# Projection stores on ScalarE's own queue, more buffers, another order of projection rows, and layer 2's S5 tables built inside the first MLP

## The chip, the cores and the metric

The kernel runs on one core of one Trainium2 chip. The metric is the device time of one execution in microseconds (us), lower is better; the time of a kernel is the median of its runs. PE is TensorE, PEld its weight loads, DVE is VectorE, ACT ScalarE, POOL GpSimd, SP SyncE, the engine that in the kernel before issues every DMA.

## What is computed

Two layers of a hybrid backbone block on 256 context and 1024 latent tokens of width 1024, all in float32. Each layer normalises and modulates its input, projects it once to four groups of heads, runs the four mixers in both directions, concatenates, projects back, adds, and then does the same with an MLP:

```python
pc, pl = split_cols(hc @ w_in), split_cols(hl @ w_in)
a = hgrn2_mixer(...)                       # gated linear attention, chunks of 16
r = retention_mixer(...)                   # rope, fixed decays, chunks of 64
g = gdn_mixer(...)                         # conv, then a triangular solve per chunk of 64
s = s5_mixer(...)                          # complex diagonal scan, 16 groups of 64 states
y = concatenate([a, r, g, s]) @ w_out
x = x + gate * y
x = x + gate2 * (square(relu(h2 @ w1)) @ w2)
```

The S5 scan of the reference is `h_t = a h_(t-1) + B u_t`, `y_t = Re(C h_t) + d u_t` for every group. It depends on the tokens only through u; B scaled by the step, the powers of a and the phasors depend on parameters alone.

## The kernel before, in words

Every dense product is made float32-exact by splitting each operand into a high and a low part and adding three matmuls (hi*hi, lo*hi, hi*lo). ACT makes the high parts, DVE or POOL the low parts (`w_lo`, `hlo`). A scheduler places the instructions: the program is written as generators with priorities, the scheduler estimates times and fixes an order for each engine, and every engine then runs its queue in that order. Work with priority (the mixers, inside `hi()`) comes as early as its inputs allow, and the "filler" of projections takes what is left of PE.

A layer has these stages. **Front**: `proj_steps` (L1642) computes rows of the input projection, each product being 24 matmuls into a PSUM tile `pj_ps` (L1661), copied to an SBUF tile `pj_z` by `evict` (L1634; every fourth copy on DVE, L1637, the others on ACT, L1639), and stored to memory from there by SP (L1666). `k.nz` = 3 buffers of pj_z, and the PSUM bank class 'mm' with 2 banks, bound how many copies are under way. The first rows are `k.rowsA`: 16, 14, 17, 15, 18, 19 are keys, queries and values of the gated DeltaNet, and row 'h' holds its decays and betas; the rest, `k.rowsB`, is filler. Beside it run `gdn_conv` (L596: convolution on DVE, L635, silu on ACT, L641, transposes to `gd_pt` on PE, L656, key products, stores of `gd_x` and `gd_tk` by SP), `gdn_stats` (L705, needs row 'h') and `s5_tables` (L1202). **GDN core**: `gdn_main` (L780) loads decays (`gd_E`, `gd_ge`, L804), forms the matrices `gd_M` and `gd_A`, solves the triangular systems on DVE (L864, L865) through the memory tile `lanes`, builds inverses (`gd_py`, L897) and steps along the chunks. **Mixers**: outputs of the DeltaNet, retention, HGRN2 and S5, woven with the next modulation. **S5**: `s5` (L1310) takes the tables `s5t` in four quarters: a product `s_px` (PE), a rotation by phasors, scans on DVE (L1380), a rotation back to `s_h`, products `s_py`; then a gelu and a gate (`s_pg`). **w_out**: `wo_ps` (L1521), first the six k-tiles of the other mixers, added on DVE (L1780), then the two S5 tiles. **MLP**: `mlp` (L1801) with `up_ps` and `dn_ps` back to back on PE; after each output tile it asks the filler for a step, and the filler is empty here.

`s5_tables(l)` (L1202) makes, in four iterations of four groups, the five tables of a quarter: EIN (DVE L1244 and L1246, POOL L1245, four transposes `s_pe` on PE, L1249), CA (L1254 to L1256), products `s_pm` (PE, L1260) that become a Toeplitz table by way of memory, and the phasors PC and PS by doubling (L1301 to L1303): each step computes the next m entries from those that are there, with the cosines on DVE and the sines on POOL, each needing the other's previous step. It is run in the front of its own layer, layer 0's as well as layer 1's.

Of the kernel before, what the change touches and what calls it, by code (L numbers as in the profile page):

```python
# [1201 lines left out]
def s5_tables(k, l):  # L1202
# [5 lines left out]
    for qi in range(4):  # L1208
        q4 = slice(4 * qi, 4 * qi + 4)
        fr, fi = (s[n].rearrange('p (l d g) -> p l d g', l=2, d=2)[:, l, :, q4] for n in ('fr', 'fi'))  # L1210
        uc, us = (s[n].rearrange('p (l d g) -> p l d g', l=2, d=2)[:, l, :, 2 * qi:2 * qi + 2] for n in ('uc', 'us'))
        own = [tile_('s5_tb', [128, b - a], f's5_tb{i}') for i, (a, b) in enumerate(zip(TBO, TBO[1:]))]
        EIN, PC, PS, CA, TP = s5_views(own)
        store = lambda i: nc.sync.dma_start(k.s5t[l][qi, :, TBO[i]:TBO[i + 1]], own[i])
        XP = tile_('s5_xp', [128, 2, 2, 4, 9], bufs=2)
# [6 lines left out]
        BR = tile_('s5_BR', [128, 2, 4, 16])
        BI = tile_('s5_BI', [128, 2, 4, 16])
        B2 = tile_('s5_B2', [128, 2, 4, 16])
        tq = tile_('s5_tq', [128, 4, 16])
        sh = [128, 4, 16]
        for d in range(2):
            f_r, f_i = bc(fr[:, d, :, None], sh), bc(fi[:, d, :, None], sh)
            V.tensor_tensor(BR[:, d], br, f_r, op=MULT)
            V.tensor_tensor(tq, bi, f_i, op=MULT)  # L1230
            V.tensor_tensor(BR[:, d], BR[:, d], tq, op=SUB)
            V.tensor_tensor(BI[:, d], bi, f_r, op=MULT)
            V.tensor_tensor(tq, br, f_i, op=MULT)
            V.tensor_tensor(BI[:, d], BI[:, d], tq, op=ADD)
# [3 lines left out]
        pts = []  # L1238
        for d in range(2):
            ee = tile_('s5_ee', [128, 4, 8, 16])  # L1240
            et = tile_('s5_et', [128, 4, 8, 16], 's5_et', 2)
            pw = lambda a: (rev(a[:, d, :, 0:8], 2) if d == 0 else a[:, d, :, 0:8])[:, :, :, None]
            sh = [128, 4, 8, 16]
# [13 lines left out]
            ps = mx(k, 's5_pm')  # L1257
            for g in range(2):
                for y in range(2):
                    nc.tensor.matmul(ps[64 * y:64 * y + 16, g * 128:g * 128 + 128], B2[:, d, 2 * g + y],  # L1260
                                     CA[:, d, 2 * g + y, 1 - d:9 - d].rearrange('p t c -> p (t c)'), start=True, stop=True)
            pts.append(ps)
            yield
        store(0)
        store(3)
        MB = tile_('s5_mb', [128, 2, 240])
        for r in Y2:
            q = slice(r.start, r.start + 16)
            f_ = pts[0][q, 0:256].rearrange('p (g c) -> p g c', g=2)
            b_ = pts[1][q, 0:256].rearrange('p (g c) -> p g c', g=2)  # L1270
            nc.scalar.activation(MB[q, :, 0:128], f_, AF.Copy)
            nc.scalar.activation(MB[q, :, 128:240], b_[:, :, 16:128], AF.Copy)
            V.tensor_tensor(MB[q, :, 112:128], MB[q, :, 112:128], b_[:, :, 0:16], op=ADD)
            for g in range(2):
                V.scalar_tensor_tensor(MB[q, g, 112:128], k.c['dmask'][q, 0:16], s['d'][q, l, 2 * qi + g:2 * qi + g + 1],
                                       MB[q, g, 112:128], op0=MULT, op1=ADD)
# [4 lines left out]
        for y in range(2):
            for g in range(2):
                t = toep[y, :, g]
                nc.sync.dma_start(TP[:, g, y], bass.AP(tensor=t.tensor, offset=t.offset,
                                                       ap=[[16, 8], list(t.ap[0]), [1, 128]]))
        G.memset(PC[:, :, :, 0], 1.0)
        G.memset(PS[:, :, :, 0], 0.0)
        G.tensor_copy(PC[:, :, :, 1], uc)
        G.tensor_copy(PS[:, :, :, 1], us)
        store(4)  # L1290
        f8 = lambda a: a.rearrange('p d g n -> p (d g) n')
        n = 1
        while n < NB - 1:
            m = min(n, NB - 1 - n)
            sh = [128, 4, m]
# [2 lines left out]
            for e, t, x, a, y, b, op in ((V, PC, xr, ar, xi, ai, SUB), (G, PS, xr, ai, xi, ar, ADD)):
                w = tile_('s5_pq', [128, 4, 64], 's5_pv' if e is V else 's5_pg')[:, :, :m]
                o = f8(t)[:, :, n + 1:n + m + 1]  # L1300
                e.tensor_tensor(o, x, a, op=MULT)  # L1301
                e.tensor_tensor(w, y, b, op=MULT)
                e.tensor_tensor(o, o, w, op=op)  # L1303
# [338 lines left out]
def proj_steps(k, l, H, rows, need_ctx):  # L1642
# [9 lines left out]
    def product(row, W, b0, bn, n, dst):  # L1652
# [214 lines left out]
def program(k):  # L1867
    from contextlib import ExitStack
    nc, tc = k.nc, k.tc
    with ExitStack() as es:  # L1870
# [62 lines left out]
        for l in range(2):  # L1933
# [104 lines left out]
def tune(k):  # L2038
# [63 lines left out]
```

## Time and profile before

| | us |
|---|---|
| median of 3 runs | 3759.85 (3757.71 to 3773.92) |
| profiled execution | 3765.0, span 3763.2, mean granted clock 0.935 |
| setup | 0 to 80 |
| layer 0: front and GDN core, mixers, S5 with w_out, MLP | 80, 717, 953, 1143 to 2030 |
| layer 1: front and GDN core, mixers, S5 with w_out, MLP | 2040, 2603, 2858, 3034 to 3763 |
| PE, DVE, ACT, POOL busy | 3337.9, 2072.9, 1110.0, 1143.3 |

The second row is one execution with the profiler on; all rows of the trace belong to it. Busy shares are means over stages, so each stage has to be read by itself. The granted clock is the share of full speed that PE was given.

### The profile page before, as it was taken

What the parts mean: (1) busy time and instruction counts of PE and PEld (TensorE: products, weight loads), DVE (VectorE), ACT (ScalarE), POOL (GpSimd) and SP (SyncE); (2) the same over time, 40 slices, a digit from 0 to 9 for tenths busy, and PEclk for the clock granted to TensorE, in tenths of its full rate; (3) what the DMA queues carried; (4) which work ended last, traced back from release to release, by engine and by line L of the source; (5) the groups of instructions that cost most, each with busy time, mean ns of one, the idle gap of its engine ahead of it and who ended that gap; (6) DMA issues with size and microseconds to landing.
All of it is one profiled execution on the core that took longest, in us unless ns stands there. A gap on an engine that the chain in (4) does not pass through costs nothing.

```text
span 3763.2 us, 60098 instructions
## 1 busy us (share of the span) xinstructions
PE 3337.9 (89%) x23367; PEld 2711.3 (72%) x23367; DVE 2072.9 (55%) x3927; ACT 1110.0 (29%) x1988; POOL 1143.3 (30%) x1198
## 2 busy tenths in 40 slices
PE   5884999897889999999997884999688799999997
PEld 3674788655767888888886784778456578888886
DVE  8958441587765334334436978421876654344445
ACT  5333212365243121121123333122462232222222
POOL 3724222364213111111112744222552231111111
PEclk8987899999999999999998997999798899999998
DMA  6547444775531111111112566534946311111111
GB/s 211 185 137 184 144 126 131 228 251 184 172 134 37 37 37 40 40 40 36 38 40 86 165 179 168 148 115 136 290 134 207 113 43 48 48 48 45 51 45 65
DMA packets 423949, 429.45 MB, mean 114 GB/s; under 512 B 185968, under 2 KB 299504, under 8 KB 422640
## 3 DMA queue, kind: packets, MB, share of 16 engines
q1 hardware_dynamic: 423664, 425.61, 36.3%
q8 instruction: 184, 3.01, 0.3%
q14 instruction: 101, 0.83, 0.1%
HBM read 313.26 MB, written 112.22 MB: 113 GB/s over the span
## 4 chain that ended last, share of the span: by engine, by line
PE 58%; DVE 11%; DMA 5%; issue 2%; ACT 2%; SPq 1%; POOL 1%; DVEq 0%; POOLq 0%; ACTq 0%
PE dn_ps L1521 21%; PE up_ps L1521 21%; PE pj_ps L1661 6%; PE wo_ps L1521 4%; DMA w_mo<-in_mod_w 1%; PE hg_pa L171 1%; DVE nm_u L1624 1%; DVE gd_y L635 1%; DVE hlo L1631 1%; PE mod_ps L1545 0%; DVE gd_tmp L864 0%; DVE s_x L1380 0%; DMA at<-a 0%; DVE hg_t L221 0%; DVE nr_acc L1593 0%
## 5 line engine op out<-in xcount | busy, mean ns | idle before, releaser
L1521 PE MATMUL dn_ps<-hid,w_hi 128*128 128x512 f32 (+1 forms) x2560 | 726.9, 373 | 9.0 <-DVE x L1833 7.7
L1833 DVE SCALAR_TENSOR_TENSOR x<-dn_ps,mod,x 128x512 f32<-128x512 f32 (+1 forms) x640 | 433.1, 695 | 323.2 <-PE dn_ps L1521 322.7
L1506 POOL TENSOR_TENSOR w_lo<-w_st,w_hi 128x512 fp32r<-128x512 f32 (+1 forms) x212 | 283.9, 1341 | 1044.1 <-ACT w_hi L1503 1016.2
L1521 PEld LDWEIGHTS dn_ps<-hid,w_hi 128*128 128x128 f32 x2560 | 462.8, 189 | 98.8 <-DVE x L1833 9.1
L1503 ACT ACTIVATE w_hi<-w_st 128x512 fp32r<-128x512 f32 (+2 forms) x408 | 249.8, 621 | 804.7 <-PE dn_ps L1521 275.7
L1521 PE MATMUL up_ps<-hlo,w_hi 128*128 128x512 f32 (+1 forms) x1280 | 475.6, 372 | 3.4 <-DVE hlo L1631 1.9
L1521 PE MATMUL up_ps<-hhi,w_hi 128*128 128x512 f32 (+1 forms) x1280 | 476.3, 373 | 2.0 <-ACT hhi L1630 2.0
L1521 PE MATMUL up_ps<-hhi,w_lo 128*128 128x512 f32 (+1 forms) x1280 | 475.8, 372 | 0.0
L1521 PE MATMUL dn_ps<-hid,w_lo 128*128 128x512 f32 (+1 forms) x1280 | 468.5, 373 | 0.0
L1661 PE MATMUL pj_ps<-hhi,w_hi 128*128 128x512 f32 (+1 forms) x960 | 366.5, 383 | 37.8 <-ACT pj_z L1639 28.0
L1661 PE MATMUL pj_ps<-hhi,w_lo 128*128 128x512 f32 (+1 forms) x960 | 365.3, 381 | 0.6 <-POOL w_lo L1506 0.6
L1661 PE MATMUL pj_ps<-hlo,w_hi 128*128 128x512 f32 (+1 forms) x960 | 363.8, 379 | 1.8 <-DVE hlo L1631 1.8
L1818 POOL TENSOR_TENSOR up_q<-up_r 128x256 f32<-128x256 f32 (+1 forms) x160 | 156.0, 976 | 565.5 <-ACT up_r L1817 476.9
L1506 DVE TENSOR_TENSOR w_lo<-w_st,w_hi 128x512 fp32r<-128x512 f32 (+1 forms) x196 | 148.6, 763 | 306.8 <-ACT w_hi L1503 298.3
L1521 PEld LDWEIGHTS up_ps<-hlo,w_hi 128*128 128x128 f32 x1280 | 242.3, 189 | 49.0 <-DVE hlo L1631 3.5
L1521 PEld LDWEIGHTS up_ps<-hhi,w_hi 128*128 128x128 f32 x1280 | 242.2, 189 | 46.2 <-ACT hhi L1630 2.8
L1521 PEld LDWEIGHTS up_ps<-hhi,w_lo 128*128 128x128 f32 x1280 | 242.0, 189 | 44.0
L1521 PEld LDWEIGHTS dn_ps<-hid,w_lo 128*128 128x128 f32 x1280 | 240.3, 189 | 45.6
L1820 DVE TENSOR_TENSOR hid<-up_q,hid 128x256 fp32r<-128x256 f32 (+1 forms) x160 | 114.3, 723 | 278.4 <-ACT hid L1819 276.0
L1661 PEld LDWEIGHTS pj_ps<-hhi,w_hi 128*128 128x128 f32 x960 | 189.7, 198 | 73.3 <-ACT pj_z L1639 29.6
L1819 ACT ACTIVATE hid<-up_q 128x256 fp32r<-128x256 f32 (+1 forms) x160 | 89.2, 584 | 423.2 <-PE dn_ps L1521 337.4
L1661 PEld LDWEIGHTS pj_ps<-hlo,w_hi 128*128 128x128 f32 x960 | 189.9, 198 | 33.1 <-DVE hlo L1631 2.4
(401 smaller groups left out, 5871.9 us busy)
## 6 DMA issues: line engine op xcount, KB each, us to landing
w_st<-in_w SPq DMA_DIRECT2D x256, 256.0 KB
w_mo<-in_mod_w SPq DMA_DIRECT2D x160, 256.0 KB
w_st<-in_w_ch SPq DMA_DIRECT2D x88, 256.0 KB
z<-pj_z SPq DMA_DIRECT2D x88, 256.0 KB
gd_KV<-kv SPq DMA_DIRECT2D x80, 192.0 KB
s_ta<-s5t SPq DMA_DIRECT2D x8, 1152.0 KB
w_mo<-in_mod_w SPq DMA_DIRECT2D x16, 512.0 KB
at<-a SPq DMA_DIRECT2D x32, 256.0 KB
```

Source lines behind the costliest of these rows:

```text
L171: m = nc.tensor.matmul(ps[Y2[c % 2], o:o + 128], key[:, a:a + 64], z[:, :, q:q + 64], start=True, stop=True)
L635: nc.vector.scalar_tensor_tensor(o, xl[:, r0 + a - 1:r1 + a - 1, w0 + b - 1:w1 + b - 1], w(a, b), o, op0=MULT, op1=ADD)
L1503: nc.scalar.activation(fl(hi), fl(st), AF.Copy)
L1506: eng.tensor_tensor(fl(lo), fl(st), fl(hi).bitcast(F32), op=SUB)
L1521: k.nc.tensor.matmul(out, w, x, start=(i + j == 0), stop=(i == n - 1 and j == 2))
L1624: nc.vector.scalar_tensor_tensor(u, X(kt)[:, sl], a, rb[:, :bn], op0=MULT, op1=MULT)
L1631: nc.vector.scalar_tensor_tensor(lo[:, sl], u, b, hi[:, sl].bitcast(F32), op0=ADD, op1=SUB)
L1661: nc.tensor.matmul(ps[:, :n], x, y, start=(kt == 0 and i == 0), stop=(kt == 7 and i == 2))
L1818: nc.gpsimd.tensor_tensor(q[:, :bn], r[:, :bn], r[:, :bn], op=MULT)
L1819: nc.scalar.activation(hi[:, sl], q[:, :bn], AF.Copy)
L1820: nc.vector.tensor_tensor(lo[:, sl], q[:, :bn], hi[:, sl].bitcast(F32), op=SUB)
L1833: nc.vector.scalar_tensor_tensor(X(m)[:, sl], ps[:, :bn], g, X(m)[:, sl], op0=MULT, op1=ADD)
```

## The change

1. `evict` gets the destination and issues the store itself: ACT's copies are stored from ACT's queue, DVE's from SP's as before.
2. `k.nz` 3 to 6, the projection's PSUM classes ('mm',) to ('mm', 'mm', 'mo') (three banks rather than two), `gd_E` 2 to 4 buffers, `gd_tk` 1 to 3 buffers. `dynamic_dma_scratch_size=1024` is passed for the program.
3. `rowsA` becomes 16, 14, 17, 15, 'h', 18, 19.
4. `s5_tables` runs eight iterations of two groups. Both directions share the scaling instructions; transposes and products share one PSUM tile; the tables are stored piece by piece; XP and BC have one buffer.
5. Layer 0's tables stay where they were; layer 1's leave its front and become the filler of layer 0's MLP, which runs with seven PSUM banks then (`DENSE2`) and not eight (`DENSE`).

```diff
-        Es = [early('gd_E', half, 2) for d in range(2)]
+        Es = [early('gd_E', half, 4) for d in range(2)]
...
-    for qi in range(4):
-        q4 = slice(4 * qi, 4 * qi + 4)
+    for qi, e in ((qi, e) for qi in range(4) for e in range(2)):
+        g2 = slice(4 * qi + 2 * e, 4 * qi + 2 * e + 2)
...
-            for g in range(4):
-                nc.tensor.transpose(ps[:, g * 128:g * 128 + 128], ee[:, g].rearrange('p s c -> p (s c)'), k.c['ident'])
+            for g in range(2):
+                nc.tensor.transpose(pt[:, g * 128:g * 128 + 128], ee[:, g].rearrange('p s c -> p (s c)'), k.c['ident'])
...
         while n < NB - 1:
             m = min(n, NB - 1 - n)
-            sh = [128, 4, m]
-            ar, ai = bc(f8(PC)[:, :, n:n + 1], sh), bc(f8(PS)[:, :, n:n + 1], sh)
-            xr, xi = f8(PC)[:, :, 1:m + 1], f8(PS)[:, :, 1:m + 1]
+            sh = [128, 2, m]
+            ar, ai = bc(PC[:, :, n:n + 1], sh), bc(PS[:, :, n:n + 1], sh)
+            xr, xi = PC[:, :, 1:m + 1], PS[:, :, 1:m + 1]
...
-def evict(k, out, ps):
+def evict(k, out, ps, dst):
     k.ec += 1
     if k.ec % k.ecm == 0:
         k.nc.vector.tensor_copy(out, ps)
+        k.nc.sync.dma_start(dst, out)
     else:
         k.nc.scalar.activation(out, ps, AF.Copy)
+        k.nc.scalar.dma_start(dst, out)
...
-        evict(k, z[:, :n], ps[:, :n])
-        nc.sync.dma_start(dst, z[:, :n])
+        evict(k, z[:, :n], ps[:, :n], dst)
...
-            k.mml = ('mm',)
+            k.mml = ('mm', 'mm', 'mo')
...
                     if l == 0:
                         hg_params(k)
-                    run(within(k, s5_tables(k, l), tb, 'mc'))
+                        run(within(k, s5_tables(k, 0), near(st, 'tb0'), 'mc'))
...
-                if k.mods[2 + l]:
+                if l == 0:
                     k.mml = DENSE2
-                    k.filler = (x for i, r in k.mods[2 + l] for x in modulation(k, i, r, k.xp, ('w_mo', 2, 1)))
+                    k.filler = within(k, s5_tables(k, 1), near(st, 'tb1'), 'mo')
...
-    k.rowsA = [16, 14, 17, 15, 18, 19, 'h']
+    k.rowsA = [16, 14, 17, 15, 'h', 18, 19]
-    k.nz = 3
+    k.nz = 6
-    k.ncv, k.ntk, k.statat = 4, 1, 3
+    k.ncv, k.ntk, k.statat = 4, 3, 3
```

The scheduler makes a new order from this. In layer 0, 71 projection matmuls stand on PE between the last `gd_pt` and the first `gd_py` before, and 253 now; in layer 1 it is 83 and 101. In layer 0's S5 stage the last quarter's `s_px` stands behind all w_out matmuls of the first six k-tiles, where before only `s_pg` did; in layer 1, where one quarter did, one and a half do now. Retention's first stage, which on PE stood among layer 0's last projections, now comes behind them. Line numbers of the changed kernel are two or three lower from the end of `s5_tables` on, and its doubling steps are L1298 to L1300.

SP's queue in layer 0's front before, around the solves' first loads (gr holds decays, kk and kv products and tokens, zr projected rows):

```order
L804 DMA gd_E<-gr_79 64x512 x2
L804 DMA gd_ge<-gr_79 64x512
L857 DMA lanes_97<-gd_M 32x16x32 x4
L804 DMA gd_ge<-gr_79 64x512 x3
L661 DMA kv_92<-gd_x 64x10x64 x7
L1666 DMA zr_73<-pj_z 128x256 x3
L1512 DMA w_st<-in_w_ch 128x512 x3
L924 DMA gd_KV<-kv_92 128x384 x4
L1666 DMA zr_73<-pj_z 128x256 x2
```

and ACT's queue of the changed kernel, at the first decays of layer 0 (each copy of pj_ps is followed by its own store):

```order
L1637 ACTIVATE pj_z_5912<-pj_ps_5887 128x256
L1638 DMA z0_69<-pj_z_5912 128x256
L820 ACTIVATE gd_E_3435<-gd_E_3435 128x512
L821 ACT_TABLE_LOAD
L821 ACTIVATE gd_E_3435<-gd_E_3435 128x512
L820 ACTIVATE gd_E_3436<-gd_E_3436 128x512
L821 ACTIVATE gd_E_3436<-gd_E_3436 128x512
L1500 ACTIVATE w_hi_6069<-w_st_6067 128x512
L839 ACTIVATE gd_ge_3457<-gd_ge_3457 128x512
L839 ACTIVATE gd_ge_3464<-gd_ge_3464 128x512
L1637 ACTIVATE pj_z_5968<-pj_ps_5943 128x512
L1638 DMA z0_69<-pj_z_5968 128x512
```

The projection stores have left SP's queue, but for DVE's copies, and stand in ACT's between the decays' activations.

DVE's queue in layer 0's S5 and w_out stage before (xp is the residual tile to which a w_out product is added, s5_x and s5_h are the scan's):

```order
L1506 TENSOR_TENSOR w_lo_10981<-w_st_10978,w_hi_10980 128x512
L1780 SCALAR_TENSOR_TENSOR xp_10874<-wo_ps_10876,mod0_122,xp_10874 128x512
L1506 TENSOR_TENSOR w_lo_10987<-w_st_10984,w_hi_10986 128x256
L1780 SCALAR_TENSOR_TENSOR xp_10909<-wo_ps_10911,mod0_122,xp_10909 128x256
L1371 TENSOR_TENSOR s5_x_9539<-s5_px_9541,s5_ta_9385 128x320
L1372 TENSOR_TENSOR s5_t1_9551<-s5_px_9546,s5_ta_9385 128x320
L1373 TENSOR_TENSOR s5_x_9540<-s5_px_9546,s5_ta_9385 128x320
L1374 TENSOR_TENSOR s5_t1_9552<-s5_px_9541,s5_ta_9385 128x320
L1375 TENSOR_TENSOR s5_x_9539<-s5_x_9539,s5_t1_9551 128x320
```

and the changed kernel there (s5_pc and s5_ps are the phasors of layer 1's tables, s5_pq their scratch):

```order
L1300 TENSOR_TENSOR s5_pc_13998<-s5_pc_13998,s5_pq_14220 128x2x16
L1298 TENSOR_TENSOR s5_pc_13998<-s5_pc_13998 128x2x32
L1299 TENSOR_TENSOR s5_pq_14228<-s5_ps_13999 128x2x32
L1300 TENSOR_TENSOR s5_pc_13998<-s5_pc_13998,s5_pq_14228 128x2x32
L1778 SCALAR_TENSOR_TENSOR xp_11323<-wo_ps_11325,mod0_130,xp_11323 128x512
L1298 TENSOR_TENSOR s5_pc_13998<-s5_pc_13998 128x2x64
L1299 TENSOR_TENSOR s5_pq_14236<-s5_ps_13999 128x128
L1300 TENSOR_TENSOR s5_pc_13998<-s5_pc_13998,s5_pq_14236 128x2x64
L1298 TENSOR_TENSOR s5_pc_13998<-s5_pc_13998 128x2x31
L1299 TENSOR_TENSOR s5_pq_14244<-s5_ps_13999 128x2x31
L1300 TENSOR_TENSOR s5_pc_13998<-s5_pc_13998,s5_pq_14244 128x2x31
```

The doubling steps of layer 1's tables have come between the additions of w_out; s5_ps is written by POOL.

PE's queue in layer 0's MLP of the changed kernel (before it, dn_ps matmuls follow one another):

```order
L1518 MATMUL dn_ps_12951<-hid_12252,w_hi_12674 128x512
L1518 MATMUL dn_ps_12951<-hid_12253,w_hi_12674 128x512
L1518 MATMUL dn_ps_12951<-hid_12252,w_lo_12675 128x512
L1253 MATMUL s5_pe_12981<-c_ident_122,s5_ee_12982 128x128 x2
L1518 MATMUL dn_ps_12990<-hid_12238,w_hi_12662 128x256
L1518 MATMUL dn_ps_12990<-hid_12239,w_hi_12662 128x256
L1518 MATMUL dn_ps_12990<-hid_12238,w_lo_12663 128x256
L1518 MATMUL dn_ps_12990<-hid_12252,w_hi_12674 128x256
L1518 MATMUL dn_ps_12990<-hid_12253,w_hi_12674 128x256
L1518 MATMUL dn_ps_12990<-hid_12252,w_lo_12675 128x256
```

A transpose of layer 1's tables has come between two products of the MLP; there are 16 pairs of transposes and 16 pairs of the tables' products (L1263) like it.

## Rows read from the trace of the kernel before

**Rows 1.** The view by windows; columns: from:to, length, busy us (instructions) per engine, clock, DMA.

```profile
core 0: us, PE busy (x) PEld busy (x) DVE busy (x) ACT busy (x) POOL busy (x), PEclk, DMA share, GB/s
240.00:300.00 60.00, 48.16 (x479) 46.98 (x475) 20.17 (x45) 20.98 (x39) 14.65 (x10) 0.91 0.57 143
300.00:340.00 40.00, 2.40 (x10) 2.00 (x10) 38.93 (x55) 15.98 (x24) 27.74 (x24) 0.50 0.65 156
717.00:953.00 236.00, 181.58 (x2066) 120.12 (x2064) 197.57 (x408) 140.00 (x240) 129.40 (x131) 0.89 0.72 229
953.00:1060.00 107.00, 105.25 (x640) 88.57 (x641) 64.51 (x126) 25.16 (x48) 20.06 (x24) 0.98 0.49 157
1060.00:1080.00 20.00, 14.43 (x47) 8.49 (x46) 10.42 (x14) 9.10 (x16) 4.24 (x3) 0.93 0.48 167
1143.00:2030.00 887.00, 877.33 (x4523) 746.55 (x4523) 384.61 (x594) 190.32 (x354) 155.24 (x149) 1.00 0.12 40
2100.00:2300.00 200.00, 136.86 (x1242) 123.09 (x1240) 172.32 (x308) 71.24 (x123) 119.47 (x138) 0.84 0.63 177
2260.00:2300.00 40.00, 2.40 (x10) 2.00 (x10) 36.33 (x47) 15.97 (x24) 26.57 (x20) 0.52 0.71 172
2930.00:2980.00 50.00, 27.62 (x144) 18.71 (x142) 31.17 (x59) 11.05 (x18) 11.44 (x13) 0.80 0.22 78
```

**Rows 2.** PE's waits, 195 to 460 us, layer 0: who ended them, us, times, longest.

```profile
PE pj_ps L1661 <- ACT pj_z L1639: 28.9, 2, 25.3
PE gd_pt L656 <- ACT gd_y L641: 18.9, 1, 18.9
```

**Rows 3.** PE's waits, 2030 to 2480 us, layer 1.

```profile
PE pj_ps L1661 <- ACT pj_z L1639: 29.6, 3, 28.4
PE gd_pt L656 <- ACT gd_y L641: 17.4, 1, 17.4
...
PE s_pe L1249 <- DVE s_ee L1246: 6.5, 3, 3.5
```

**Rows 4.** Timeline of SP's queue, 318 to 346 us: start, length, line, what is issued.

```profile
327.54 1.09 SPq L804 DMA_DIRECT2D gd_E<-gr  x2
...
329.77 1.98 SPq L857 DMA_DIRECT2D lanes<-gd_M  x4
...
333.62 5.84 SPq L661 DMA_DIRECT2D kv<-gd_x  x7
339.51 1.82 SPq L1666 DMA_DIRECT2D zr<-pj_z  x3
```

**Rows 5.** Timeline of ACT over the same stretch; brackets: idle before it, what ended that.

```profile
342.82 0.74 ACT L1639 ACTIVATE pj_z<-pj_ps 128x256 f32<-128x256 f32 x2 [6.19 <-DMA zr<-pj_z]
```

**Rows 6.** Groups by line, DVE, 2030 to 2320 us: count, busy us, mean ns, idle before.

```profile
L1301 DVE TENSOR_TENSOR s_tb<-s_tb 128x4 f32<-128x4 f32 (+7 forms) x32 | 13.3, 416 | 5.7 <-POOL s_tb L1288 5.2
L1302 DVE TENSOR_TENSOR s_pq<-s_tb 128x4 f32<-128x4 f32 (+7 forms) x32 | 13.0, 406 | 0.8 <-POOL s_tb L1303 0.7
...
L1303 DVE TENSOR_TENSOR s_tb<-s_tb,s_pq 128x4 f32<-128x4 f32 (+7 forms) x32 | 8.3, 261 | 0.4
...
L1273 DVE TENSOR_TENSOR s_mb<-s_mb,s_pm 16x32 f32<-16x32 f32 x8 | 1.4, 177 | 0.1
```

**Rows 7.** Groups by line, POOL, the same stretch.

```profile
L1301 POOL TENSOR_TENSOR s_tb<-s_tb 128x4 f32<-128x4 f32 (+7 forms) x32 | 20.3, 636 | 22.1 <-DVE s_tb L1303 9.0 <-DVE s_BI L1234 7.5 <-DVE s_tq L1233 2.0
...
L1303 POOL TENSOR_TENSOR s_tb<-s_tb,s_pq 128x4 f32<-128x4 f32 (+7 forms) x32 | 17.4, 544 | 1.9
```

**Rows 8.** One line, L1301, 80 to 240 us: shortest, median, longest ns.

```profile
L1301 DVE TENSOR_TENSOR s_tb<-s_tb x32: 154/227/1294, 88.3 to 219.5; 128x4 f32<-128x4 f32 x4, 128x8 f32<-128x8 f32 x4, 128x16 f32<-128x16 f32 x4, 128x32 f32<-128x32 f32 x4
L1301 POOL TENSOR_TENSOR s_tb<-s_tb x32: 210/406/1461, 88.5 to 220.1; 128x4 f32<-128x4 f32 x4, 128x8 f32<-128x8 f32 x4, 128x16 f32<-128x16 f32 x4, 128x32 f32<-128x32 f32 x4
```

**Rows 9.** Timeline of PE, 2126.5 to 2131.5 us.

```profile
2127.61 0.62 PE L1260 MATMUL s_pm<-s_tb,s_B 128*16 128x128 f32 x8
2128.16 0.66 PE L1249 MATMUL s_pe<-c_ident,s_ee 128*128 128x128 f32 x4
2128.57 0.48 PE L1661 MATMUL pj_ps<-hhi,w_lo 128*128 128x512 f32 x1
```

More of the change, by code (lines that the diff above doesn't have):

```diff
@@ L1207, in s5_tables @@
     tile_ = lambda nm, sh, tag=None, bufs=1: k.tp.tile(sh, F32, name=nm, tag=tag or nm, bufs=bufs)
-    for qi in range(4):
-        q4 = slice(4 * qi, 4 * qi + 4)
[L1210 to L1215, printed above, removed]
+    ldg = lambda n: s[n].rearrange('p (l d g) -> p l d g', l=2, d=2)[:, l]
@@ new lines, in s5_tables @@
+    for qi, e in ((qi, e) for qi in range(4) for e in range(2)):
+        g2 = slice(4 * qi + 2 * e, 4 * qi + 2 * e + 2)
+        fr, fi = (ldg(n)[:, :, g2] for n in ('fr', 'fi'))
+        uc, us = (ldg(n)[:, :, 2 * qi + e] for n in ('uc', 'us'))
+        EIN = tile_('s5_ein', [128, 2, 2, 128])
+        PC, PS = tile_('s5_pc', [128, 2, NB]), tile_('s5_ps', [128, 2, NB])
+        CA = tile_('s5_ca', [128, 2, 2, 9, 16])
+        TP = tile_('s5_tp', [128, 2, 128])
+        out = s5_views([k.s5t[l][qi, :, a:b] for a, b in zip(TBO, TBO[1:])])
+        XP = tile_('s5_xp', [128, 2, 2, 2, 9])
@@ L1216, in s5_tables @@
         for i in range(2):
             nc.sync.dma_start(XP[:, i].rearrange('p d g n -> p d (g n)'),
-                              k.s5x[:, i].rearrange('p (l d g) n -> p l d (g n)', l=2, d=2)[:, l, :, 36 * qi:36 * qi + 36])
-        BC = tile_('s5_bc', [128, 4, 4, 16], bufs=2)
-        nc.sync.dma_start(BC, k.I['s5bc'][:, :, l, q4])
+                              k.s5x[:, i].rearrange('p (l d g) n -> p l d (g n)', l=2, d=2)[:, l, :, 9 * g2.start:9 * g2.stop])
+        BC = tile_('s5_bc', [128, 4, 2, 16])
@@ L1221, in s5_tables @@
+        nc.sync.dma_start(BC, k.I['s5bc'][:, :, l, g2])
         br, bi, cr, ci = (BC[:, i] for i in range(4))
[L1222 to L1234, printed above, removed]
+        BR = tile_('s5_BR', [128, 2, 2, 16])
@@ new lines, in s5_tables @@
+        BI = tile_('s5_BI', [128, 2, 2, 16])
+        B2 = tile_('s5_B2', [128, 2, 2, 16])
+        tq = tile_('s5_tq', [128, 2, 2, 16])
+        sh = [128, 2, 2, 16]
+        f_r, f_i = bc(fr[:, :, :, None], sh), bc(fi[:, :, :, None], sh)
+        b_r, b_i = bc(br[:, None], sh), bc(bi[:, None], sh)
+        V.tensor_tensor(BR, b_r, f_r, op=MULT)
+        V.tensor_tensor(tq, b_i, f_i, op=MULT)
+        V.tensor_tensor(BR, BR, tq, op=SUB)
+        V.tensor_tensor(BI, b_i, f_r, op=MULT)
+        V.tensor_tensor(tq, b_r, f_i, op=MULT)
@@ L1235, in s5_tables @@
+        V.tensor_tensor(BI, BI, tq, op=ADD)
         fl = lambda a: a.rearrange('p d g c -> p (d g c)')
@@ L1237, in s5_tables @@
         nc.scalar.activation(fl(B2[Y2[1]]), fl(BI[Y2[1]]), AF.Copy, scale=-1.0)
-        pts = []
+        ps = mx(k, 's5_pe')
+        pm = ps[:, 256:512].rearrange('p (d c) -> p d c', d=2)
         for d in range(2):
-            ee = tile_('s5_ee', [128, 4, 8, 16])
-            et = tile_('s5_et', [128, 4, 8, 16], 's5_et', 2)
+            ee = tile_('s5_ee', [128, 2, 8, 16])
+            et = tile_('s5_et', [128, 2, 8, 16], 's5_et')
             pw = lambda a: (rev(a[:, d, :, 0:8], 2) if d == 0 else a[:, d, :, 0:8])[:, :, :, None]
-            sh = [128, 4, 8, 16]
+            sh = [128, 2, 8, 16]
             V.tensor_tensor(ee, bc(pw(XP[:, 0]), sh), bc(BR[:, d, :, None, :], sh), op=MULT)
@@ L1246, in s5_tables @@
             V.tensor_tensor(ee, ee, et, op=ADD)
-            ps = mx(k, 's5_pe')
-            for g in range(4):
-                nc.tensor.transpose(ps[:, g * 128:g * 128 + 128], ee[:, g].rearrange('p s c -> p (s c)'), k.c['ident'])
-            nc.scalar.activation(EIN[:, d].rearrange('p g c -> p (g c)'), ps, AF.Copy)
+            pt = ps[:, 0:256]
+            for g in range(2):
+                nc.tensor.transpose(pt[:, g * 128:g * 128 + 128], ee[:, g].rearrange('p s c -> p (s c)'), k.c['ident'])
+            nc.scalar.activation(EIN[:, d].rearrange('p g c -> p (g c)'), pt, AF.Copy)
+            yield
             pw = lambda a: (rev(a[:, d], 2) if d == 0 else a[:, d])[:, :, :, None]
-            sh = [128, 4, 9, 16]
-            ct = tile_('s5_ct', sh, 's5_et', 2)
+            sh = [128, 2, 9, 16]
+            ct = tile_('s5_ct', sh, 's5_et')
             V.tensor_tensor(CA[:, d], bc(pw(XP[:, 0]), sh), bc(cr[:, :, None, :], sh), op=MULT)
@@ L1256, in s5_tables @@
             V.tensor_tensor(CA[:, d], CA[:, d], ct, op=ADD)
[L1257 to L1262, printed above, removed]
+            for y in range(2):
+                nc.tensor.matmul(pm[64 * y:64 * y + 16, d], B2[:, d, y],
+                                 CA[:, d, y, 1 - d:9 - d].rearrange('p t c -> p (t c)'), start=True, stop=True)
             yield
-        store(0)
-        store(3)
-        MB = tile_('s5_mb', [128, 2, 240])
+        nc.sync.dma_start(out[0][:, :, 2 * e:2 * e + 2], EIN)
+        nc.sync.dma_start(out[3][:, :, 2 * e:2 * e + 2].rearrange('p d g n c -> p d (g n c)'), CA.rearrange('p d g n c -> p d (g n c)'))
+        MB = tile_('s5_mb', [128, 240])
         for r in Y2:
             q = slice(r.start, r.start + 16)
[L1269 to L1276, printed above, removed]
+            nc.scalar.activation(MB[q, 0:128], pm[q, 0], AF.Copy)
+            nc.scalar.activation(MB[q, 128:240], pm[q, 1, 16:128], AF.Copy)
+            V.tensor_tensor(MB[q, 112:128], MB[q, 112:128], pm[q, 1, 0:16], op=ADD)
+            V.scalar_tensor_tensor(MB[q, 112:128], k.c['dmask'][q, 0:16], s['d'][q, l, 2 * qi + e:2 * qi + e + 1],
+                                   MB[q, 112:128], op0=MULT, op1=ADD)
         toep = k.toep[k.ti % len(k.toep)]
@@ L1281, in s5_tables @@
         for y in range(2):
[L1282 to L1291, printed above, removed]
+            t = toep[y]
+            nc.sync.dma_start(TP[:, y], bass.AP(tensor=t.tensor, offset=t.offset, ap=[[16, 8], list(t.ap[0]), [1, 128]]))
+        nc.sync.dma_start(out[4][:, e], TP)
+        yield
+        G.memset(PC[:, :, 0], 1.0)
+        G.memset(PS[:, :, 0], 0.0)
+        G.tensor_copy(PC[:, :, 1], uc)
+        G.tensor_copy(PS[:, :, 1], us)
         n = 1
@@ L1294, in s5_tables @@
             m = min(n, NB - 1 - n)
-            sh = [128, 4, m]
-            ar, ai = bc(f8(PC)[:, :, n:n + 1], sh), bc(f8(PS)[:, :, n:n + 1], sh)
-            xr, xi = f8(PC)[:, :, 1:m + 1], f8(PS)[:, :, 1:m + 1]
[L1298 to L1303, printed above, removed]
+            sh = [128, 2, m]
+            ar, ai = bc(PC[:, :, n:n + 1], sh), bc(PS[:, :, n:n + 1], sh)
+            xr, xi = PC[:, :, 1:m + 1], PS[:, :, 1:m + 1]
+            for en, t, x, a, y, b, op in ((V, PC, xr, ar, xi, ai, SUB), (G, PS, xr, ai, xi, ar, ADD)):
+                w = tile_('s5_pq', [128, 2, 64], 's5_pv' if en is V else 's5_pg')[:, :, :m]
+                o = t[:, :, n + 1:n + m + 1]
+                en.tensor_tensor(o, x, a, op=MULT)
+                en.tensor_tensor(w, y, b, op=MULT)
+                en.tensor_tensor(o, o, w, op=op)
             n *= 2
-        store(1)
-        store(2)
+        nc.sync.dma_start(out[1][:, :, e], PC)
+        nc.sync.dma_start(out[2][:, :, e], PS)
         yield
@@ L1887, in program @@
         k.lanes = [k.dp.tile([3, 128, 32, 32], F32, name=f'lanes{i}') for i in range(6)]
-        k.toep = [k.dp.tile([2, 16, 2, 240], F32, name=f'toep{i}') for i in range(8)]
+        k.toep = [k.dp.tile([2, 16, 240], F32, name=f'toep{i}') for i in range(16)]
         k.pace = lambda i, m: pace(k, i, m)
@@ L1944, in program @@
             with ExitStack() as st:
-                gv, gc, su, tb = (near(st, f'{n}{l}') for n in ('gv', 'gc', 'su', 'tb'))
+                gv, gc, su = (near(st, f'{n}{l}') for n in ('gv', 'gc', 'su'))
                 with hi():
@@ L2086 @@
     from concourse.bass_utils import run_bass_kernel_spmd as _run
-    nc = _bacc.Bacc("TRN2", target_bir_lowering=False, num_devices=1)
+    nc = _bacc.Bacc("TRN2", target_bir_lowering=False, num_devices=1, dynamic_dma_scratch_size=1024)
     arrays, k = {}, K()
```

## The prediction, on record before the run

> **What bounds the kernel now.** I read the windows by stage first, then PE's waits in the two worst stretches, then the timelines of the queues that those waits name, and last the groups by line of the work that the change moves. In the windows [rows 1] the reader should see that the stages have different limits. In layer 0's MLP (1143 to 2030 us) PE is busy 877.33 of 887 us at a granted clock of 1.00: there only PE's own work counts, and anything added to PE is paid. Between 300 and 340 us PE is busy 2.40 us of 40, and again 2.40 of 40 between 2260 and 2300 in layer 1, each time at about the lower of its two levels (0.50 and 0.52), while DVE is busy for 38.93 and 36.33 us. PE's waits say on what: 18.9 us on the last transpose of a convolved row and 25.3 us on a projection copy in layer 0 [rows 2], 17.4 and 28.4 us in layer 1 [rows 3]. These two pairs, 44.2 and 45.8 us, are the largest holes in the kernel.
>
> Why does PE wait 25.3 us on a copy of 0.37 us? ACT's copy pair starts at 342.82 and had been held by a buffer whose store had not gone out [rows 5]. SP's queue shows the reason: up to 339.51 it is busy with loads and stores that wait for DVE, POOL and the decays, among them four stores of gd_M at 329.77 and seven of gd_x at 333.62, and only then come three projection stores [rows 4]. With three pj_z buffers and two PSUM banks the whole projection stops behind SP's order of issue. But DVE is at its end too in that stretch, and the solves need it, so the projection runs earlier without the solves necessarily doing so.
>
> **The change, part by part.** The sum is against the profiled execution, 3765.0 us, which is 5.2 us above the median of the runs.
>
> *Layer 0's front.* ACT's copies go out on ACT's queue, six buffers and a third PSUM bank stand behind them, and the program order now has 253 projection matmuls, not 71, between the last gd_pt and the first gd_py. Those 182 more are worth 18 to 35 us: 0.10 us each by the stretch 240 to 300 (48.16 us for 479), 0.194 by the MLP (877.33 for 4523) [rows 1]. Most are the long form, so the upper end is nearer: **-35 us** (bounds -10 and -44, the whole hole). Row 'h' ahead of 18 and 19 brings the statistics earlier: DVE is busy only 20.17 of 60 us between 240 and 300, so 40 us of idle DVE can take table work there. That table work grows: halved iterations double the doubling chain's instructions, 96 more on DVE at no less than 0.154 us [rows 8], so about 15 us, and as many on POOL at 0.21, about 20. Both fit the idle DVE and I cost them at nothing here; without that cover the solves start 15 us later.
> The trace gives 0.154 us as the shortest of these; the Trainium skill (Perfetto Trace Analysis, Optimizing Scalar/DVE Operations) counts about 60 ns of data access per DVE instruction on SBUF and advises larger grouped operations, against the halving; by its figure it would be an estimated 6 us.
>
> *Layer 1's front.* The same hole of 45.8 us, and here the tables leave altogether: DVE loses 15 groups from L1301's 13.3 us down to L1273's 1.4, in all 87.1 us [rows 6], in a stretch where it is busy 172.32 of 200 [rows 1], and POOL's three lines of the doubling chain, 58.0 us, from 20.3 to 17.4 [rows 7]. PE loses its waits on s_ee, 6.5 us [rows 3], and its table products: 12 instructions in 0.96 us from 2127.61 to 2128.57 [rows 9], eight such groups, 8 us. The granted clock in 2100 to 2300 is 0.84; outside the hole, by subtracting the 40 us at 0.52, it is 0.92. About 5 us return from that. 45.8 + 6.5 + 8 + 5 = **-65 us** (bounds -25, if the solves hold the end, and -80).
>
> *The displaced projections.* Work that runs earlier no longer covers the mixers: in 717 to 953 PE is already idle for 54 us [rows 1], and the order has retention's first stage now after the projections. **+5** (0 to +15).
>
> *Layer 0's S5 and output projection.* Here I see the main price. The order shows that the phasor doubling chains of layer 1's tables are taken early and stand in DVE's queue between the evictions of w_out. Their cost is the 34.6 us of DVE (13.3 + 13.0 + 8.3) [rows 6] plus 15 for the halving, 50 us, and 78 on POOL, alternating. In 953 to 1060 DVE has 42.5 us left and PE is busy for 105.25 of 107 [rows 1]: DVE is filled, and behind each chain step wait the evictions that free PE's banks. **+10** (0 to +50). The last S5 quarter also moves behind the w_out matmuls, as layer 1 has it now: there PE idles 22.4 of 50 us (2930 to 2980), here 5.6 of 20 (1060 to 1080) [rows 1]. **+17** (0 to +25). In layer 1 half a quarter more goes the same way: **+10** (0 to +22).
>
> *Layer 0's MLP.* PE takes the 8 us of table products. DVE has 502 us idle there and POOL 732 [rows 1], which hides the tables' other work; if a transpose comes to PE before its operand, PE stands. Each such wait is 2.2 us by the 6.5 in three [rows 3], and there are 32 places, so 0 to 70; I take 5, since the scheduler put whole down blocks between them. **+13**. Seven PSUM banks instead of eight cost nothing, hidden by DVE being idle more than half the time; if it were not, it would show as PE waiting on x.
>
> *Stores on ACT's queue* cost ACT some 0.6 us of issue each by SP's three in 1.82 [rows 4]. ACT is busy 15.98 of 40 us in the hole [rows 1], so this is hidden unless a copy waits for PE ahead of a decay exponential.
>
> Sum: -35 - 65 + 5 + 10 + 17 + 10 + 13 = **-45 us**, 3720 by the profiled execution and, 5 less, **3715** by the median.
>
> **The rivals.** *More is kept*: the scans and evictions absorb the later losses (+5, +10, +17, +10 and the 5 of waits fall away): -92, or 3668. For it speaks that DVE's share in 953 to 1060 is 60%; against it that layer 1 shows the exposed S5 already.
> *The front's end is set by the solves*: DVE is at 97% and 91% in both holes, so the projection only ends sooner and the mixers wait. Then the fronts give 15 and 45, together -60 + 55 = -5, or 3755.
> *The queue is no limit*: the transfers themselves are late, with the DMA share at 0.65 and 0.71 in the holes. Only the extra buffers and bank help, four products of 24 matmuls, 10 to 19 us a front, say 14; with layer 1's other 19 it is -47 + 55 = +8, or 3768. Against it: the stores landed within 4 us of being issued.
> The Trainium skill (DMA: Bandwidth & Descriptors, Issuing engines are not separate DMA queues) states the rule behind this: all queues share the same 16 engines, and a second issuer saves only issue time. The trace agrees in part: what was lost was 5.84 us of SP's own issuing and its waits [rows 4].
> *Slower, one mechanism*: an in-order DVE queue that waits for POOL in the moved tables. Every doubling step needs POOL's half, whose mean is 0.636 us against DVE's 0.416 [rows 6, 7]. If w_out's stretch takes +40 instead of +10, and the MLP's 32 transposes each wait 2.2 us, 70 instead of 5, the sum is -45 + 95 = +50, or 3810. It decides for slower once these two come to 64 us more than I set.
>
> **How the numbers follow.** A measurement of this kernel can tell about 0.5%, 19 us, from no change: 3741 and 3779 are the bounds. Chances: my forecast 0.45 (its own range 3685 to 3745, faster nine times in ten), more kept 0.17, solves 0.18 (a quarter of it faster, the rest the same), queue 0.08 (the same), slower 0.12. So faster 0.405 + 0.17 + 0.045 = 0.62, same 0.26, slower 0.12. The range 3660 to 3780 leaves out the slow rival and a corner of the large gain.
>
> **What would show it.** Right: no PE wait over 10 us on pj_z or gd_pt in either front; projections of layer 1 ended 60 us or more earlier by the stage's length; DVE nearly full in layer 0's output projection, with the doubling lines there; PE waiting on s_px, s_py or s_h after the last w_out matmul of its first six tiles; the MLP longer by 8 to 20 us. Wrong: a hole of 20 us or more that stays in either front; a shorter S5 stage; an MLP longer by over 40 us, with PE waiting on s_ee.

## The result, and the profile after

The changed kernel takes 3785.26 us (median of 6 runs, 3780.88 to 3791.41) against 3763.98 for the kernel before (6 runs): a ratio of 1.0058, interval 1.0045 to 1.0071. It is slower by 0.6%, where faster by 45 us was forecast. Its profiled execution has a span of 3785.1 us. Layers are counted from 0 here: the title's layer 2 is layer 1.

The windows of the changed kernel that answer to [rows 1]; columns as there:

```profile
300.00:340.00 40.00, 30.08 (x137) 24.43 (x135) 30.24 (x43) 14.19 (x23) 25.06 (x17) 0.91 0.87 225
901.00:1104.00 203.00, 147.13 (x827) 118.65 (x825) 150.63 (x411) 46.35 (x88) 101.26 (x268) 0.84 0.46 144
1143.00:2030.00 887.00, 882.74 (x4580) 746.20 (x4580) 411.29 (x701) 202.78 (x405) 181.09 (x177) 1.00 0.15 46
2100.00:2300.00 200.00, 153.15 (x1279) 139.76 (x1280) 125.33 (x188) 75.92 (x120) 69.55 (x39) 0.85 0.58 155
2240.00:2280.00 40.00, 5.17 (x36) 4.47 (x35) 36.18 (x49) 12.73 (x20) 32.04 (x16) 0.63 0.79 216
```

The hole at 300 to 340 is filled (30.08 us of PE instead of 2.40), layer 1's DVE is relieved (125 instead of 172 in 2100 to 2300), yet in 2240 to 2280 PE stands again. In 901 to 1104, where layer 0's S5 and w_out run, DVE is busy for 150.63 of 203 us and so not full. PE's waits in 195 to 460 us and in 2060 to 2480 us, the longest of each:

```profile
PE pj_ps L1660 <- ACT w_hi L1500: 20.7, 1, 20.7
```

```profile
PE pj_ps L1660 <- ACT w_hi L1500: 32.1, 1, 32.1
```

What is left of the holes of [rows 2, 3] has another name: not the copy of a result, but the splitting of the next weights, 20.7 us where there were 44.2, and 32.1 where there were 45.8. SP's queue and ACT in layer 0, with the waits in brackets:

```profile
346.25 2.37 SPq L804 DMA_DIRECT2D gd_E<-gr  x4
...
351.85 1.23 SPq L1509 DMA_DIRECT2D w_st<-in_w_ch  x2
```

```profile
356.16 1.37 ACT L1500 ACTIVATE w_hi<-w_st 128x512 fp32r<-128x512 f32 x2 [2.52 <-DMA w_st<-in_w_ch]
```

The weight loads of the projections come after the decays' loads in SP's order, as the stores did in [rows 4]. And DVE, which was to have the decays early, waits for them: their loads are issued at 297.28 us, behind stores of the tables (293.07) and of the values (293.94):

```profile
304.00 1.49 DVE L819 TENSOR_TENSOR gd_E<-gd_E,gd_gp 128x512 f32<-128x512 f32 x2 [15.42 <-DMA gd_E<-gr]
```

Where the time went is read from the first and last starts of a stage's products. The last w_out product of layer 0 (the second start; before, then changed):

```profile
L1521 PE MATMUL wo_ps<-alo,w_hi x192: 275/392/629, 954.5 to 1125.2; 128*128 128x512 f32 x128, 128*128 128x256 f32 x64
```

```profile
L1518 PE MATMUL wo_ps<-alo,w_hi x192: 274/392/632, 935.7 to 1156.8; 128*128 128x512 f32 x128, 128*128 128x256 f32 x64
```

Layer 0 up to there loses 32 us, although w_out begins 19 us earlier. The first MLP, to its last dn_ps, takes 925 us instead of 918 (1156.8 to 2082.3, 1125.2 to 2042.8), 8 more. Layer 1, from there to the end of the span, takes 1702.8 instead of 1720.4: 18 less. Together +22.

What fills the S5 and w_out stage is seen in DVE's groups, 860 to 1160 us of the changed kernel, and in its and POOL's waits there:

```profile
L1298 DVE TENSOR_TENSOR s_pc<-s_pc 128x2 f32<-128x2 f32 (+3 forms) x64 | 19.4, 303 | 19.8 <-POOL s_pc L1287 18.4
L1300 DVE TENSOR_TENSOR s_pc<-s_pc,s_pq 128x2 f32<-128x2 f32 (+3 forms) x64 | 17.0, 265 | 1.6
...
L1299 DVE TENSOR_TENSOR s_pq<-s_ps 128x2 f32<-128x2 f32 (+3 forms) x64 | 15.0, 234 | 5.6 <-POOL s_ps L1300 4.2 <-POOL s_ps L1288 0.9
```

```profile
DVE s_pc L1298 <- POOL s_pc L1287: 18.4, 6, 4.1
```

```profile
POOL s_pc L1285 <- DMA s5t<-s_pc: 19.0, 6, 4.1
```

The doubling chains work 51.4 us (19.4 + 17.0 + 15.0), and before them DVE stands for 27 us more (19.8 + 1.6 + 5.6). The longest share is a round trip: POOL may clear the phasor tile s_pc for the next iteration only when its store has landed, because the tile has one buffer. One such place on POOL and then on DVE:

```profile
1007.84 0.10 POOL L1285 MEMSET s_pc<- 128x2 f32 x1 [3.99 <-DMA s5t<-s_pc]
```

```profile
1008.10 0.16 DVE L1298 TENSOR_TENSOR s_pc<-s_pc 128x2 f32<-128x2 f32 x1 [4.14 <-POOL s_pc L1287]
```

The scans and the additions of w_out queue behind it on DVE, and PE's longest wait in that stage is the next S5 product's:

```profile
PE s_px L1362 <- DVE s_x L1370: 16.1, 3, 9.0
```

### The profile page after: what moved, and what is told of

Read it like the earlier page. It is cut to its first block, busy times and chain, and to the rows that moved or that the text cites. A ratio compares the mean times of both kernels' runs of the same rounds, so it can differ in the third digit from the quotient of the medians.

```text
span 3785.1 us, 60804 instructions
## 1 busy us (share of the span) xinstructions
PE 3352.6 (89%) x23367; PEld 2714.1 (72%) x23367; DVE 2088.5 (55%) x4199; ACT 1118.1 (30%) x2052; POOL 1185.9 (31%) x1454
## 5 line engine op out<-in xcount | busy, mean ns | idle before, releaser
L1500 ACT ACTIVATE w_hi<-w_st 128x512 fp32r<-128x512 f32 (+1 forms) x408 | 249.6, 621 | 761.2 <-PE dn_ps L1518 243.2
L1660 PE MATMUL pj_ps<-hhi,w_hi 128*128 128x512 f32 (+1 forms) x960 | 361.4, 378 | 31.0 <-ACT w_hi L1500 20.7
L1660 PEld LDWEIGHTS pj_ps<-hhi,w_lo 128*128 128x128 f32 x960 | 185.9, 194 | 32.7 <-POOL w_lo L1503 2.4
```

Of the source, the lines that this page charges most:

```text
L1500: nc.scalar.activation(fl(hi), fl(st), AF.Copy)
L1660: nc.tensor.matmul(ps[:, :n], x, y, start=(kt == 0 and i == 0), stop=(kt == 7 and i == 2))
```

## The experiments

Two theories at the start. **A**: layer 1's doubling chains, taken early, cost layer 0's S5 and w_out stage. **B**: the loss is made in layer 0's front, where the solves come late. Times are medians, ratios are against the kernel before in runs on the same chip. Differences between two variants are of medians, in part from different chips, on which the kernel before differed by up to 4 us. Times within a run are those of its one profiled execution.

**Tables back in layer 1** (stores, buffers and order kept):

```diff
+                    run(within(k, s5_tables(k, l), near(st, f'tb{l}'), 'mc'))
...
-                    k.filler = within(k, s5_tables(k, 1), near(st, 'tb1'), 'mo')
```

> The changed kernel with layer 1's tables put back into layer 1's front (eight small iterations there, the MLP with eight PSUM banks and no filler). Theory A, the doubling chains taken early cost layer 0's S5 and w_out stage: that stage is 12 to 30 us shorter than in the changed kernel, the MLP 8 us shorter, the first MLP ends at 2040 to 2062 us instead of 2082; layer 1's front is longer by 20 to 40 us, and the total is 3770 to 3800. Theory B, the loss comes from layer 0's front alone (solves late by the order of SP's queue): the S5 and w_out stage keeps its length, the first MLP ends at 2070 to 2080, total 3790 to 3815.

3788.01 us, ratio 1.0051 (1.0034 to 1.0068). The last w_out product:

```profile
L1518 PE MATMUL wo_ps<-alo,w_hi x192: 279/390/632, 922.9 to 1123.1; 128*128 128x512 f32 x128, 128*128 128x256 f32 x64
```

It starts 34 us earlier, and the first MLP ends at 2042.7: A's numbers for layer 0, with a little more than it asked for. Layer 1 then takes 1733 us (2042.7 to 3775.9) instead of 1703. The move does save 30 us there, and loses them again earlier. (The profiled execution, 3777.69 us, was the fastest of five, 10 under the median.)

**The tables held behind the MLP's own work**, by an ordering edge on DVE and POOL (k.last holds the MLP's latest POOL and DVE instructions):

```diff
...
-                next(k.filler, None)
+                with k.tc.issue_after(k.last[0].ins), k.tc.issue_after(k.last[1].ins):
+                    next(k.filler, None)
```

> The changed kernel, with the moved tables kept behind the first MLP's own work on DVE and POOL, so that no doubling chain can stand in the S5 and w_out stage. Theory A: that stage is 12 to 30 us shorter, total 3755 to 3775. Theory B: the stage is within 5 us of the changed kernel's, total 3780 to 3790. If the tables then come too late inside the MLP, PE waits there for s_ee and the MLP is longer than 935 us.

3737.32 us, ratio 0.9922 (0.9907 to 0.9938): 48 us below the changed kernel, more than A asked for. The last w_out product:

```profile
L1518 PE MATMUL wo_ps<-alo,w_hi x192: 274/391/628, 930.0 to 1123.7; 128*128 128x512 f32 x128, 128*128 128x256 f32 x64
```

33 us of the gain lie before it; most of the rest is in layer 1 (1681.8 us against 1702.8), whose order came out otherwise and was not taken apart. Layer 0's part comes with layer 0's front as late as in the changed kernel (first gd_py at 373.4 and 372.1 us). So B falls: the late solves are made up for in the mixers, whose HGRN2 products begin earlier (694 instead of 738 us).

**The move alone, and the move held, in the kernel before**:

> The kernel before with the new tables code, layer 1's tables in the first MLP, and nothing else of the change. If the move is worth what layer 1's front showed: first MLP 8 us longer, layer 1's front 40 to 65 us shorter, S5 and w_out of layer 0 longer by 10 to 30, total 3725 to 3755. If the solves set the front's end: 3755 to 3775. If the tables cost more than they free: over 3775.

> The kernel before with the new tables code and layer 1's tables in the first MLP, kept behind that MLP's own DVE and POOL work; nothing else of the change. Theory A (the doubling chains taken early are what costs the move its gain): layer 0's w_out ends at 1118 to 1132 us instead of 1148 as in the move without the hold, and the total is 3735 to 3755. Rival (the move lengthens the mixers or the MLP by itself): w_out ends at 1140 or later, total 3765 to 3775.

3772.39 us, 1.0014 (1.0003 to 1.0024), and 3746.20 us, 0.9944 (0.9929 to 0.9959). The hold is worth 26 us without anything else of the change; the last w_out product starts at 1132.6 instead of 1147.2, just past the edge of what A said. But this pair does not repeat A's stage. In the move alone the scheduler takes the chains earlier still, in the mixers; DVE's groups, 600 to 900 us:

```profile
L1298 DVE TENSOR_TENSOR s_pc<-s_pc 128x2 f32<-128x2 f32 (+3 forms) x64 | 17.5, 273 | 15.1 <-POOL s_pc L1287 13.7
```

There w_out begins 20 us later than before (974.8 instead of 954.5) and takes as long (172 us, 171 before). Chains that are taken early cost time in either stage, and the hold ends both.

The move alone also shows what layer 1 gains from it: 1690.0 us instead of 1720.4, though its two waits on pj_z and gd_pt are still there (27.4 and 18.2 us at the longest). Its total is that of the branch in which the solves set the front's end, not of the one in which the move is worth the whole hole.

**Two buffers for the phasors**, with the chains left where they are (the freed scratch halved to make room):

```diff
-        PC, PS = tile_('s5_pc', [128, 2, NB]), tile_('s5_ps', [128, 2, NB])
+        PC, PS = tile_('s5_pc', [128, 2, NB], bufs=2), tile_('s5_ps', [128, 2, NB], bufs=2)
```

> The changed kernel with two buffers instead of one for the phasor tiles s5_pc and s5_ps; the doubling chains stay where they are in the S5 and w_out stage. If the round trips of the tiles' stores are what DVE pays there (18.4 us of waits on POOL's copy, which waits on the store): these waits fall below 5 us, w_out ends 10 to 20 us earlier than 1157, total 3765 to 3776. If the chains' own work fills DVE: the waits fall, w_out ends within 5 us of 1157, total 3780 to 3788.

3753.77 us, ratio 0.9973 (0.9962 to 0.9983), 31 us below the changed kernel and faster than before. DVE's groups, 860 to 1140 us:

```profile
L1298 DVE TENSOR_TENSOR s_pc<-s_pc 128x2 f32<-128x2 f32 (+7 forms) x64 | 18.8, 295 | 4.0 <-POOL s_pc L1287 1.8 <-POOL s_ps L1286 1.0
L1299 DVE TENSOR_TENSOR s_pq<-s_ps 128x2 f32<-128x2 f32 (+3 forms) x64 | 17.1, 267 | 4.8 <-POOL s_ps L1300 4.3
...
L1300 DVE TENSOR_TENSOR s_pc<-s_pc,s_pq 128x2 f32<-128x2 f32 (+3 forms) x64 | 14.8, 232 | 1.2
```

The last w_out product:

```profile
L1518 PE MATMUL wo_ps<-alo,w_hi x192: 276/392/632, 938.9 to 1135.3; 128*128 128x512 f32 x128, 128*128 128x256 f32 x64
```

The work is the same, 50.7 us, the idle before it 10 instead of 27, and that product starts 21 us earlier, though w_out begins 3 us later. The total fell by more than was expected of either branch (3765 or more), and not all of it is the buffers': layer 1 takes 1682.0 us here, 21 less than in the changed kernel, as in the held variant. The chains do not run there; the order came out otherwise (the wait on w_hi is 39.1 us in layer 0's front and 7.3 in layer 1's). In layer 0 the round trips are most of the price; the other 12 us go when the chains leave the stage (1135.3 to 1123.7), which is ascribed to their work and not shown apart.

**ACT's stores alone, and with six buffers and a third bank**, in the kernel before:

> The kernel before, with nothing changed but the stores of ACT's copies on ACT's queue. If the store order on SP was what held the projections (the prediction's reading): the holes of 25 to 28 us shrink by half or more, total 3735 to 3755. If the holes are kept by late weights or by the solves: a hole of 20 us or more stays in each front under another name, total 3755 to 3775. If the copies on ACT now hold up the decays: over 3775.

> The kernel before with ACT's stores on ACT's queue, six pj_z buffers and the third PSUM bank. If buffers were what ACT's stores lacked: the holes fall below 10 us in each front, total 3735 to 3760. If the weights behind the decays in SP's queue hold the projections whatever the stores do: PE waits 18 to 32 us on w_hi in each front, total 3770 to 3800.

3792.36 us, 1.0078 (1.0050 to 1.0105), and 3756.39 us, 0.9964 (0.9951 to 0.9977). By itself the other queue is a loss of 24 us; with the buffers it gains 12. With three pj_z buffers the waits on w_hi are 22.0 and 21.6 us in the two fronts: the hole is renamed there already. Late decays are hardly the reason for the loss: the first gd_py comes 4 us later. Layer 1 takes 22 us longer (1742.6 instead of 1720.4), and its GDN core ends only 4 us later, counted from the first MLP's end; why the mixers lose the rest was not settled. With six buffers and the third bank the waits on w_hi stay, 20.9 and 27.7 us, which was expected to go with 3770 us or more. The kernel is faster nevertheless, by layer 0 (last w_out product at 1110.1 instead of 1125.2): the length of the hole does not tell the time.

**Stores back on SP, and the row order back**, both in the held variant:

> The held variant of the changed kernel (3737 us) with all projection stores back on SP's queue, six buffers and three banks kept. If ACT's stores are a loss by themselves (24 us in the kernel before): total 3710 to 3730. If they pay once there are more buffers: total 3745 to 3770, with PE waits on pj_z again. If only the buffers count: 3730 to 3745.

> The held variant with the row of decays and betas last again, as before. If the earlier row brings the solves forward: the first solve and gd_py of layer 0 come 10 us later or more, total 3745 to 3760. If it makes the solves late (372 us against 360 before): gd_py at 360 to 366, total 3720 to 3735. If its order does not matter: 3732 to 3742.

3768.28 us, 1.0005 (0.9995 to 1.0016): there the stores on ACT are worth 31 us, and with them on SP PE waits for pj_z again (27.0 and 20.6 us at the longest). 3736.56 us, 0.9917 (0.9902 to 0.9932): the row order is worth nothing in sum. With the old one the first gd_py comes at 359.7 instead of 373.4 and the last w_out product 11 us earlier (1112.8), but layer 1 takes 12 us longer (1694.1 instead of 1681.8).

**Fewer buffers with the held move** (gd_E 2, gd_tk 1, old row order):

> The kernel before with the held move, ACT's stores, six pj_z buffers and three banks, but two gd_E buffers, one gd_tk buffer and the old row order. The held move gave -22 and stores with buffers -12 by themselves; if they add up, total 3730 to 3738 and the further buffers and the row order are worth nothing. If those buffers carry part of it: 3740 to 3755.

3746.99 us, 0.9950 (0.9933 to 0.9967). It differs from the held variant with the old row order by gd_E and gd_tk alone, which so carry about 10 us; the gains of 22 and 12 don't add up without them.

**The projections' weights loaded from ACT's queue**, in the held variant:

```diff
-    k.nc.sync.dma_start(st, src)
+    (k.nc.scalar if shape[-1] in (256, 272) or shape[1:] == [4, 128] and k.mml == ('mm', 'mm', 'mo') else k.nc.sync).dma_start(st, src)
```

> The held variant with the projection's weight loads issued by ACT instead of SP. If SP's order holds the weights behind the decays' loads: PE's wait of 21 us on w_hi in layer 0's front falls below 8 us, total 3710 to 3732. If ACT's own order holds their splitting: the wait stays at 15 us or more, total 3732 to 3750, or more where a load that waits for its buffer holds ACT's copies up.

3729.57 us, ratio 0.9901 (0.9881 to 0.9921), the best version. PE's wait in layer 0's front, 195 to 460 us:

```profile
PE pj_ps L1660 <- ACT w_hi L1500: 3.4, 1, 3.4
```

That SP's order held the weights is shown by the wait that went, 21.1 to 3.4 us. But a hole of 21 us in layer 0 and one of 7 in layer 1 gave back some 8 us at the end.

**S5's loads from ACT's queue**, in the changed kernel and with the version above:

> The changed kernel with S5's loads (inputs and tables) issued by ACT instead of SP; the doubling chains stay where they are. In the changed kernel layer 1's first S5 product comes 46.7 us after HGRN2's last score product, and 18.8 us before the change. If SP's order holds S5's loads behind the mixers' last output stores: this falls below 30 us, layer 1 is 10 to 25 us shorter, and layer 0's S5 stage still ends late, total 3755 to 3778. If something else holds S5 (its inputs, DMA bandwidth): the 46.7 us stay at 40 or more, total 3778 to 3795.

> The held variant with the projection's weight loads and S5's loads both issued by ACT: the candidate for the best version. If each removes its own wait behind SP: 5 to 20 us below the 3730 of the weights alone, 3710 to 3725. If S5's loads on ACT hold ACT's own work up: 3730 to 3750.

3788.34 us, 1.0063 (1.0047 to 1.0080), and 3740.46 us, 0.9934 (0.9917 to 0.9951). The reason to try was that in the changed kernel layer 1's first S5 product comes 47 us after HGRN2's last score product, and 19 before. It starts at 2837.9 as before this edit (2837.8): the loads are issued 5 us earlier, at 2819.13 instead of 2824.45, after the gates' activations that now stand before them, and the product does not move. SP's order is not shown to hold S5 there, what does was not found, and on ACT the loads cost 11 us in the better version.

## Why the prediction was wrong

- **Two steps failed.** From the forecast -45 to the +22 of the traces it is 67 us: 35 in layer 0 up to its last w_out product (-3 forecast, +32 measured), 37 in layer 1 (-55 forecast, -18 measured), less 5 in the MLP.
- **The first is the +10 for the doubling chains in w_out's stage.** Their place and their work were right: 50 us were set for DVE, 51.4 measured. The price was not: 34 us (1156.8 against 1123.1 with the tables back in layer 1), 24 more than was set and within the term's own bounds. The sum weighed busy time against idle time (42.5 us) and took DVE to be filled; it has 52 of 203 us left. It left out that the chain has a wait of its own: one buffer, and a store that must land before the next iteration, 18.4 us of waiting on POOL's copy in an in-order queue with the scans behind. With a second buffer 21 of the 34 us went.
- **The second is the -65 for layer 1's front, which took PE's whole hole as time to be won.** Layer 1 takes 1720.4 us before, 1690.0 with the move alone, 1733.2 with everything but the move and 1702.8 with both: the move is worth 30 us, and the rest of the change costs 13, whichever is added first (one execution of each, the third 10 us under its median and with the halved iterations in the front). The GDN core ends 560 us after the first MLP before, 532 with the move alone, whose hole is still there, 562 with everything but the move, and 521 with both. So taking the tables out of the front counted, as it does if DVE's solves set the end, and shortening the hole by itself did not. Of the hole 32.1 us came back as a wait on w_hi (a hole of 20 us or more was named as a sign of being wrong), and the granted clock in 2100 to 2300 stayed at 0.85, 0.84 before, so that the 5 us set for it are not seen. Of the 40 us by which the GDN core ends earlier, 22 were lost again up to the end. The +10 set for S5 is part of that; the rest was not settled.
- **The slower rival had the right engine and half of the place.** Its +40 for w_out's stretch was nearer to the 34 than the sum's +10. DVE waited for POOL in the moved tables, but mostly for POOL's clearing of a tile, not for the sines (4.2 us), and only in w_out's stage. In the MLP the table products hardly waited: 0.3 and 1.1 us before PE's two groups of them. In the move alone, with the chains in the mixers, the wait for the sines was the larger one, 18.9 us.
- **Layer 0's front, -35: wrong sign at the solves, right for PE.** The hole at 300 to 340 was filled, but the last GDN output came 20 us later (647 instead of 627) and HGRN2's products began 41 us earlier. The end of the stage didn't care: without the chains the last w_out product starts at 1123.1, 2 us earlier than before, where -35 + 5 + 17 = -13 was forecast. Which of these three terms was off was not taken apart.
- **"The queue is no limit" and the reading of SP's order.** SP's order was a cause, but of more than the stores: weights, decays and stores share it. Taking one kind away lets the next one wait. In the held variant the stores on ACT are worth 31 us, and the weights on ACT took PE's wait on w_hi from 21.1 to 3.4 us. The Trainium skill (DMA: Bandwidth & Descriptors, Issuing engines are not separate DMA queues) says that a second issuer saves only issue time, which it calls usually small; no run here splits the 31 us into issue time and what the queue's order held back.
- **The MLP, +13: 8 measured**, the table products as counted and no waits of note. **The row order** and the four gd_E buffers were costed at nothing: right in sum for the first, while gd_E and gd_tk carry about 10 us.

## What to carry to other kernels

Work that is moved into a "free" stage may be scheduled earlier than the stage, as soon as its inputs allow; read from the new order where it lands, and hold it there by an edge if its new neighbours share an in-order queue. Price a moved chain by its waits as well as its busy time: how often it goes round, what frees its buffer, and what stands behind it. A hole on the busiest engine is not yet time to be won: ask which engine ends the stage. Where one queue's order makes a hole, list everything that is issued behind the blocking load, for removing one item only shows the next.

## What was not expected of the hardware

POOL waited up to 4.1 us for a store of s_pc, a tile of 128 x 320 values, to free its single buffer, 19.0 us in six times. Moving the projection stores from SP to ACT without more buffers made the kernel 24 us slower, and with six buffers and a third bank 12 faster: the sign of a queue's change depended on the buffers behind it.
